# A hybrid attention and mLSTM layer on Trainium2: output stored patch by patch, and a smaller scratch for dynamic DMA descriptors

## Chip, cores and metric

The kernel runs on one core of a Trainium2 chip (TRN2). The metric is the device time of one execution in microseconds (us), the median of several runs. Before the change it is 1314.05 us, median of 3 runs (1313.41 to 1314.33).

## What is computed

One layer of a bidirectional encoder, in float32: x has 2048 tokens of 1024 features. The reference, cut to what matters:

```python
mod = silu(c) @ w_ada + b_ada
shift, scale, gate = split(mod, 3)
h = rmsnorm(x, norm_w) * (1 + scale) + shift
proj = h @ w_in + b_in                      # columns split between two head groups
na_out = neighbourhood_attention(q, k, v, rpb) * silu(na_z)   # 8 heads of 64, 8x16 window
qk = silu(short_conv(concat([ml_q, ml_k])))
hm = (mlstm_forward + mlstm_backward) * sigmoid(ml_o)         # 4 heads of 128
ml_out = layernorm_per_head(hm) * ml_norm_w * silu(ml_z)
y = concat([na_out, ml_out]) @ w_out
out = rmsnorm(x + gate * y, final_norm_w)   # (1, 2048, 1024)
```

The attention sees the 2048 tokens as a grid of 32 rows by 64 columns. A query attends to a window of 8 rows and 16 columns around it.

## The kernel before

The work is in two phases. Phase 1 builds h, runs the input projection, the convolution and the mLSTM, and leaves queries, values, gates and the mLSTM branch in DRAM scratch tensors (`d_qna`, `d_vna`, `d_zna`, `d_mix`); the keys stay in SBUF. Matrix products are split into three passes of high and low parts (`hhi`, `hlo`, `whi`, `wlo`).

Phase 2 (`phase2`, from L1399) goes over 16 patches of the grid. A patch is 8 rows by 16 columns, 128 queries, which are the 128 partitions of a tile. The host lays the residual x out by patches as well (`x_p`), so that a patch's x is loaded as one block of 128 rows. A patch has four units of two heads each, and a slot handles two units, so that a patch takes two slots. A slot (`slot`, L1741) issues by hand, in this order: scores (`pS`, L1538), softmax (L1546, L1547, L1558), the products with the values of the slot before (`pO`, L1581), transposes of the probabilities (`pT`, L1566), and between them pieces of the output projection of an earlier patch (`y`, L1626), which fill TensorE's queue. The order of all engines is fixed by the code (`manual_schedule`).

POOL's queue carries phase 2's loads: value chunks (`v`, L1466, one transfer for each grid row of a chunk), the gates (`load_z`, L1476, into `zs` and `gtile`), the mLSTM branch (`load_m`, L1483, into `whi_a` or `wlo_a`), and the residual (`load_x`, L1493, into `xr`). Each transfer of POOL waits for the eighth transfer before it on that queue, since eight semaphores are used in turn. SP's queue carries the bias tables (L1510) and, from the fourth pair on, the queries (L1448).

The output projection of a patch (`outproj`, L1603) adds y to x (L1631), squares it (L1633), and has `scale` (L1652) and `store` (L1666) work out the final norm. For 15 patches, `store` scales the patch on VectorE (L1668) and issues one store of 512 KB from POOL (L1669). The last patch (`end`) is handled in halves, to shorten the end: ScalarE scales the left 512 columns and its queue stores them (L1659, L1660), VectorE scales the right 512 and SP's queue stores them (L1661, L1662).

The destination of these stores is a piece of the output in token order, `og[8 * pr : 8 * pr + 8, 16 * pc : 16 * pc + 16, :]` (L1423, L1650): 8 grid rows, which lie 64 tokens apart, of 16 tokens each.

Of the kernel before, what the change touches and what calls it, by code (L numbers as in the profile page):

```python
# [16 lines left out]
D = 1024  # L17
T = 2048
# [3 lines left out]
GRID_W = 64  # L22
# [36 lines left out]
class Kernel:  # L59
# [1339 lines left out]
    def phase2(self):  # L1399
        nc = self.nc  # L1400
# [16 lines left out]
        for b in range(16):  # L1417
            pr, pc = divmod(b, 4)
# [1 line left out]
            rpc = ROWS_PER_CHUNK[nr, nkc]  # L1420
            nch = -(-nr // rpc)
            geo.append((pr, pc, nr, nkc, nr * nkc, rpc, nch))
        og = self.out[0].rearrange("(r c) d -> r c d", c=GRID_W)  # L1423
        vg = self.d_vna.rearrange("(r c) d -> r c d", c=GRID_W)
        L = {b: {} for b in range(16)}
        fnw = []
# [51 lines left out]
        def mix_parts(b):  # L1478
            m = mixes[pos[b] % 2]
            return [m[:, i * D : (i + 1) * D].rearrange("p (c q) -> p c q", c=8) for i in range(2)]  # L1480

        def load_m(b):
            nc.gpsimd.dma_start(mix_parts(b)[1][:, 4:, :].bitcast(F32), self.d_mix[b])  # L1483

        def load_x(b):
            src = self.x_p[b]
            if b == last_b:
                L[b]["x"] = [p.tile([P, 512], F32, tag="v", bufs=6, name=f"xr_{b}_{i}") for i in range(2)]
                for i, x in enumerate(L[b]["x"]):
                    nc.gpsimd.dma_start(x, src[:, 512 * i : 512 * i + 512])  # L1490
                return
            x = flat(self.raw.tile([P, 4, 256], F32, tag=f"raw{pos[b] % 2}", name=f"xr_{b}"))
            nc.gpsimd.dma_start(x, src)  # L1493
            L[b]["x"] = [x[:, 512 * i : 512 * i + 512] for i in range(2)]
            L[b]["row"] = x
# [107 lines left out]
        def outproj(b):  # L1603
            lb = L[b]
            hi, lo = mix_parts(b)
            end = b not in after
            pieces = [slice(0, 512), slice(512, 768), slice(768, 1024)] if end else [slice(0, 512), slice(512, 1024)]
            ssq = few.tile([P, 4], F32, tag="var", bufs=2, name=f"fss_{b}")
            halves = ((4, 5, 6, 7), (0, 1), (2, 3)) if b == b0 else ((4, 5, 6, 7), (0, 1, 2, 3))
            parts = [(i, ks) for ks in halves for i in range(2)]  # L1610
            if end:
                parts += [(2, ks) for ks in halves]
            nxt = after.get(after.get(b))
            ys = {}
            for i, ks in parts:
                cs = pieces[i]
                if i not in ys:
                    finish()
                    ys[i] = self.pp.tile([P, 512], F32, tag="pp", name=f"y_{b}_{i}")[:, : cs.stop - cs.start]
                y = ys[i]  # L1620
                assert (b, ks[0] // 4) in split
                if ks[0] == 0 and i == 0 and nxt is not None:
                    load_m(nxt)
                for k in ks:
                    for n, (m, w) in enumerate(((hi, wohi), (hi, wolo), (lo, wohi))):
                        nc.tensor.matmul(y, m[:, k, :], w[k][:, cs], start=(k == 4 and n == 0), stop=(k == 3 and n == 2))  # L1626
                        if k != 3 or n < 2:
                            yield
                if ks[-1] == 3:
                    x = lb["x"][cs.start // 512][:, cs.start % 512 : (cs.stop - 1) % 512 + 1]  # L1630
                    nc.vector.tensor_add(x, x, y)  # L1631
                    at = i + 3 - len(pieces)
                    square = lambda x=x, y=y, at=at: nc.scalar.activation(y, x, AF.Square, accum_out=ssq[:, at : at + 1])  # L1633
                    if end:
                        square()
                    else:
                        self.squares.append(square)
                    if end and i == 1:
                        nc.vector.tensor_add(ssq[:, 1:2], ssq[:, 0:1], ssq[:, 1:2])
                        nc.vector.tensor_scalar(ssq[:, 1:2], ssq[:, 1:2], 1.0 / D, EPS, ALU.mult, ALU.add)  # L1640
                    if end:
                        nc.gpsimd.tensor_tensor(x, x, fnw[0][:, cs].bitcast(F32), ALU.mult)
                    yield
            L.pop(b)
            done.append(b)
            rst = few.tile([P, 1], F32, tag="rst", bufs=2, name=f"frs_{b}")
            var = few.tile([P, 1], F32, tag="fvar", bufs=2, name=f"fvar_{b}")

            pr, pc = divmod(b, 4)
            to = og[8 * pr : 8 * pr + 8, 16 * pc : 16 * pc + 16, :]  # L1650

            def scale():  # L1652
                if not end:
                    nc.vector.tensor_scalar(ssq[:, 1:2], ssq[:, 1:2], 1.0 / D, EPS, ALU.mult, ALU.add)
                nc.vector.scalar_tensor_tensor(var, ssq[:, 2:3], 1.0 / D, ssq[:, 1:2], ALU.mult, ALU.add)
                self.rsqrt(few, rst, var, f"f{b}")
                if end:
                    left, right = lb["x"]
                    nc.scalar.activation(left, left, AF.Copy, scale=rst)  # L1659
                    nc.scalar.dma_start(to[:, :, : D // 2], left)  # L1660
                    nc.vector.tensor_scalar(right, right, rst, None, ALU.mult)  # L1661
                    nc.sync.dma_start(to[:, :, D // 2 :], right)  # L1662
                else:
                    self.todo += [lambda: None, store]

            def store():  # L1666
                x = lb["row"]
                nc.vector.scalar_tensor_tensor(x, x, rst, fnw[0].bitcast(F32), ALU.mult, ALU.mult)  # L1668
                nc.gpsimd.dma_start(to, x)  # L1669
                if nxt not in (None, last_b):  # L1670
                    self.reloads += [lambda: None, lambda: load_x(nxt)]

            if end:
                self.between.append(scale)
            else:
                self.squares.append(lambda: self.between.append(scale))
# [54 lines left out]
        def finish():  # L1731
            while self.squares:
                self.squares.pop(0)()

        def mixed(b, half):
            mix_high(b, half)
            mix_low(b, half)
            if half:
                self.queue.append(outproj(b))
# [67 lines left out]


_INS = ['x', 'x_p', 'x_t', 'cT', 'c_row', 'w_mod', 'w_gt', 'b_ada', 'norm_w', 'w_main', 'w_gate', 'b_col', 'b_row', 'b_gate', 'conv_w', 'conv_b', 'rpb', 'ml_w', 'w_out', 'fnw']
_OUTS = [((1, 2048, 1024), 'float32')]  # L1810


def layout(inputs):
# [71 lines left out]
```

## Time and profile before

| what | value |
|---|---|
| median of 3 runs | 1314.05 us |
| the profiled execution, its own time | 1315.58 us |
| its span, first to last instruction | 1313.8 us |
| mean granted TensorE clock | 0.987 |
| moved by DMA | 263.31 MB, mean 200 GB/s |
| HBM read, written | 177.28 MB, 92.72 MB |

All numbers of the profile are from one execution, whose time is 1.8 us above its span and 1.5 us above the median of the runs. Times of day count from the span's start. PE is TensorE (matmul), PEld its weight load, DVE is VectorE, ACT ScalarE, POOL GpSimd, SP SyncE; SPq and ACTq are the DMA-issuing side of those engines. A row such as "x15, 512.0 KB, 6.8" in the list of DMA issues is a count, the size of one transfer, and the median time from issue to landing in us.

### The profile page before, as it was taken

Reading aid. Unit: us, or ns where it says so; the run is one execution under the profiler, and the core shown is the slowest. Engines: PE = TensorE matmul, PEld = TensorE weight load, DVE = VectorE, ACT = ScalarE, POOL = GpSimd, SP = SyncE. Lnnn points to the kernel's source line nnn. Section 1 sums busy time; section 2 is a strip of 40 time slices with the busy share of each in tenths; the row PEclk is TensorE's granted clock in tenths of the full one; section 3 lists DMA queues with packets and bytes.
Section 4 is the critical chain, followed back from the end, with each engine's and each line's share of the span. In section 5 each row is a group of like instructions: output and inputs, shape, how many; then the busy total and the mean of one; then the engine's idle time right before and its main releaser. Section 6 shows DMA issues by size and latency. Waiting matters only on the chain.

```text
span 1313.8 us, 23067 instructions
## 1 busy us (share of the span) xinstructions
PE 1282.8 (98%) x8170; PEld 1103.1 (84%) x8170; DVE 793.4 (60%) x2394; ACT 531.3 (40%) x1172; POOL 260.6 (20%) x380
## 2 busy tenths in 40 slices
PE   9889999999999999999999999999999999999996
PEld 8889999999888887888888888888777778778785
DVE  5876452112567565166678878767447576766663
ACT  4444243542234222223323323333256555565551
POOL 1400002432000000111212002122305423324431
PEclk7989999999999999999999999999999999999998
DMA  9799955997778764645756767656678756656651
GB/s 363 250 282 305 262 188 152 228 234 202 195 183 186 170 149 110 193 131 165 207 153 209 245 184 215 214 157 183 206 252 261 203 182 194 209 181 194 190 178 48
DMA packets 220662, 263.31 MB, mean 200 GB/s; under 512 B 25463, under 2 KB 165623, under 8 KB 220548
## 3 DMA queue, kind: packets, MB, share of 16 engines
q1 hardware_dynamic: 142526, 189.92, 50.1%
q10 hardware_dynamic: 63270, 35.75, 9.6%
q0 software_dynamic: 14752, 36.17, 9.4%
q8 instruction: 65, 1.06, 0.3%
q14 instruction: 49, 0.40, 0.1%
HBM read 177.28 MB, written 92.72 MB: 206 GB/s over the span
## 4 chain that ended last, share of the span: by engine, by line
PE 80%; issue 4%; DVE 3%; DMA 3%; ACT 1%; POOL 1%; POOLq 0%; ACTq 0%; SPq 0%; DVEq 0%
PE pq L1046 23%; PE y L1626 11%; PE pc L605 4%; PE pc L606 4%; PE pc L604 4%; PE pO L1581 3%; PE pT L1566 3%; PE pvo L604 3%; PE pvo L606 3%; PE pvo L605 3%; PE pS L1538 2%; PE pv L606 2%; PE pv L605 2%; PE pv L604 2%; PE pi L1285 2%
## 5 line engine op out<-in xcount | busy, mean ns | idle before, releaser
L1046 PE MATMUL pq<-hhi,whi_a 128*128 128x512 f32 x512 | 208.4, 407 | 0.9 <-ACT u L951 0.9
L1046 PE MATMUL pq<-hlo,whi_a 128*128 128x512 f32 x512 | 208.2, 407 | 0.0
L1046 PE MATMUL pq<-hhi,wlo_a 128*128 128x512 f32 x512 | 206.7, 404 | 0.0
L1046 PEld LDWEIGHTS pq<-hhi,whi_a 128*128 128x128 f32 x512 | 96.8, 189 | 17.5 <-ACT u L951 1.3
L1046 PEld LDWEIGHTS pq<-hhi,wlo_a 128*128 128x128 f32 x512 | 96.7, 189 | 16.9 <-POOL wlo_a L1020 0.4
L1046 PEld LDWEIGHTS pq<-hlo,whi_a 128*128 128x128 f32 x512 | 96.8, 189 | 16.1 <-issue 0.5
L1020 POOL TENSOR_TENSOR wlo_a<-rawq,whi_a 128x1024 fp32r<-128x1024 f32 x19 | 45.6, 2399 | 293.3 <-ACT whi_a L1019 281.6
L1568 ACT ACTIVATE pt<-pT 96x384 f32<-96x384 f32 (+3 forms) x128 | 65.8, 514 | 87.3 <-PE pT L1566 85.1
L1547 ACT ACTIVATE pbuf<-pbuf,mn 128x480 f32<-128x480 f32 (+5 forms) x128 | 75.9, 594 | 47.8 <-DVE mn L1546 47.8
L1626 PE MATMUL y<-hhi,whi_a 128*128 128x512 f32 x256 | 91.6, 420 | 0.5 <-ACT whi_a L1596 0.5
L1626 PE MATMUL y<-hhi,wlo_a 128*128 128x512 f32 (+1 forms) x272 | 90.6, 399 | 0.2 <-ACT y L1633 0.2
L1466 POOL DMA_DIRECT2D v<-d_vna x158 | 81.8, 523 | 45.0 <-PE pO L1581 17.0
L1288 ACT ACTIVATE num<-px,gtile 128x129 f32<-128x129 f32 x120 | 38.3, 366 | 113.1 <-PE px L1283 80.4
L1546 DVE CUSTOM_DVE_ANT_0 pbuf<-pS,tab 128x480 f32<-128x480 f32 (+5 forms) x128 | 61.8, 539 | 32.3 <-PE pS L1538 32.3
L1307 POOL TENSOR_TENSOR hm<-hm,ck 128x128 f32<-128x128 f32 x64 | 27.5, 429 | 250.6 <-DVE hm L1306 218.5
L1566 PEld LDWEIGHTS pT<-ident,pbuf 128*128 128x128 f32 (+2 forms) x416 | 51.1, 136 | 23.2 <-ACT pt L1568 5.7
L1566 PE MATMUL pT<-ident,pbuf 128*128 128x128 f32 (+2 forms) x416 | 67.0, 274 | 3.0 <-DVE pbuf L1558 2.1
L604 PE MATMUL pvo<-whi_b,hhi 128*128 128x256 f32 x224 | 63.9, 285 | 0.7 <-DVE gates L678 0.7
L606 PE MATMUL pvo<-whi_b,hlo 128*128 128x256 f32 x224 | 63.1, 282 | 0.0
L605 PE MATMUL pvo<-wlo_b,hhi 128*128 128x256 f32 x224 | 63.1, 282 | 0.0
L893 ACT ACTIVATE dec<-dec,gtile 128x128 f32<-128x128 f32 x128 | 41.3, 391 | 49.2 <-POOL dec L886 46.4
L676 DVE TENSOR_TENSOR stvo<-pvo,brow 128x256 f32<-128x256 f32 x60 | 24.8, 419 | 57.6 <-PE pvo L606 44.9
(334 smaller groups left out, 3371.8 us busy)
## 6 DMA issues: line engine op xcount, KB each, us to landing
ck<-d_ck SPq DMA_DIRECT2D x64, 384.5 KB, 3.5
rawq<-in_w_main_dram SPq DMA_DIRECT2D x28, 512.0 KB, 4.5
raw<-in_w_main_dram SPq DMA_DIRECT2D x18, 512.0 KB, 6.1
kv<-d_ck SPq DMA_DIRECT2D x64, 128.5 KB, 2.8
dec<-d_mneg SPq DMA_DIRECT2D x32, 256.0 KB, 5.5
d_ck<-dec ACTq DMA_DIRECT2D x32, 256.0 KB, 7.2
d_qna<-qst ACTq DMA_DIRECT2D x32, 256.0 KB, 4.6
d_ck<-stvo SPq DMA_DIRECT2D x15, 514.0 KB, 4.8
```

Of the source, the lines that this page charges most:

```text
L604: nc.tensor.matmul(ps, lhi(k), rhi(k), start=(k == 0), stop=False)
L605: nc.tensor.matmul(ps, lhi(k), rlo(k), start=False, stop=False)
L606: self.mark = nc.tensor.matmul(ps, llo(k), rhi(k), start=False, stop=(k == KT - 1))
L893: nc.scalar.activation(t[:, o, :], t[:, o, :], AF.Exp, bias=self.cols["g"][:, d, h, c : c + 1])
L1020: (eng or nc.gpsimd).tensor_tensor(lo[:, :, cs], raw, hi[:, :, cs].bitcast(F32), ALU.subtract)
L1046: self.mark = nc.tensor.matmul(patch_ps(ps) if patch else ps, w, self.htok(h, g, k, patch), start=(k == 0 and n == 0), stop=(k == KT - 1 a ...
L1466: queue.dma_start(chunks[key][r * nkc : (r + 1) * nkc, :], rows[r])
L1546: nc.vector.tensor_tensor_reduce(pt[:, :nk], ps, tabs[place[u]][:, j * nk : (j + 1) * nk], 1.0, 3e38, ALU.add, ALU.min, mn)
L1547: nc.scalar.activation(pt[:, :nk], pt[:, :nk], AF.Exp, bias=mn, scale=-1.0, accum_out=sums[:, j : j + 1])
L1566: nc.tensor.transpose(ps[:cs, i, :], U[u][j][:, i * cs : (i + 1) * cs], self.ident)
L1568: nc.scalar.activation(t[:cs, :nch, :], ps[:cs, :nch, :], AF.Copy)
L1626: nc.tensor.matmul(y, m[:, k, :], w[k][:, cs], start=(k == 4 and n == 0), stop=(k == 3 and n == 2))
```

## The change

The output tensor gets the shape of the patches: 16 patches of 128 rows by 1024. Every store then names the patch's block, 128 rows one behind the other in DRAM, and the host puts the patches in their places after the run, outside the timed part. This concerns 17 DMA instructions: 15 from POOL, which now name 128x1024 where they named 8x16x1024, and the last patch's two, 128x512 where they named 8x16x512. The bytes are the same, and so is what each partition sends.

The second part sets the size of the scratch for dynamic DMA descriptors, an area of SBUF at address 0, to 4096 bytes of each partition. The parameter was left at its default before, 16384. Tiles that were placed from the end of that area upward now lie 12288 bytes lower; the freed room is not used.

No instruction moves: on each of the five engines the program has the same instructions in the same order with the same waits, and only the shape of those 17 transfers differs.

```diff
-        og = self.out[0].rearrange("(r c) d -> r c d", c=GRID_W)
...
-            pr, pc = divmod(b, 4)
-            to = og[8 * pr : 8 * pr + 8, 16 * pc : 16 * pc + 16, :]
+            to = self.out[b]
...
-                    nc.scalar.dma_start(to[:, :, : D // 2], left)
+                    nc.scalar.dma_start(to[:, : D // 2], left)
                     nc.vector.tensor_scalar(right, right, rst, None, ALU.mult)
-                    nc.sync.dma_start(to[:, :, D // 2 :], right)
+                    nc.sync.dma_start(to[:, D // 2 :], right)
...
-_OUTS = [((1, 2048, 1024), 'float32')]
+_OUTS = [((16, 128, 1024), 'float32')]
...
-    nc = _bacc.Bacc("TRN2", target_bir_lowering=False, num_devices=1)
+    nc = _bacc.Bacc("TRN2", target_bir_lowering=False, num_devices=1, dynamic_dma_scratch_size=4096)
...
-    return r.results[0]["out_0_dram"]
+    return r.results[0]["out_0_dram"].reshape(4, 4, 8, 16, D).transpose(0, 2, 1, 3, 4).reshape(1, T, D)
```

## The prediction

> **What bounds the kernel now.** I read the page's engine rows first, then a table by stage (busy time of each engine between chosen moments), because the change touches only the last stage. The first row is from the page; the others have, after the stretch and its length, the busy time of PE, PEld, DVE, ACT and POOL, the granted clock, the DMA share and GB/s.
>
> ```profile
> PE 1282.8 (98%) x8170; PEld 1103.1 (84%) x8170; DVE 793.4 (60%) x2394; ACT 531.3 (40%) x1172; POOL 260.6 (20%) x380
> ```
> ```profile
> 1020.50:1123.00 102.50, 102.50 (x774) 81.75 (x773) 67.91 (x225) 57.71 (x151) 34.12 (x64) 1.00 0.65 195
> 1123.00:1205.00 82.00, 82.00 (x620) 65.25 (x619) 55.18 (x180) 47.16 (x120) 25.34 (x47) 1.00 0.64 196
> 1205.00:1302.30 97.30, 97.10 (x706) 78.65 (x704) 59.38 (x201) 47.14 (x132) 34.94 (x63) 1.00 0.52 155
> 1302.30:1313.80 11.50, 0.00 (x0) 0.00 (x0) 2.68 (x11) 1.23 (x3) 0.72 (x1) 0.67 0.16 46
> ```
>
> The first patch's store is issued at 1020.6 us. From there to 1302.3 us TensorE is busy in 281.6 of 281.8 us at full clock, so nothing that the patch stores do in that stretch holds it up. The waits of PE from 1020 us on have one row in all:
>
> ```profile
> PE y L1626 <- ACT y L1633: 0.2, 1, 0.2
> ```
>
> What TensorE does not cover is the last 11.5 us. The timeline of the end gives its order (start, duration, engine, line):
>
> ```profile
> 1302.00 0.28 PE L1626 MATMUL y<-hhi,wlo_a 128*128 128x256 f32 x1
> ...
> 1305.50 0.72 ACT L1659 ACTIVATE xr<-xr,frs 128x512 f32<-128x512 f32 x1 [2.16 <-issue]
> 1305.53 0.49 DVE L1661 TENSOR_SCALAR xr<-xr,frs 128x512 f32<-128x512 f32 x1
> 1306.04 0.68 SPq L1662 DMA_DIRECT2D out_dram<-xr  x1
> 1306.26 0.69 ACTq L1660 DMA_DIRECT2D out_dram<-xr  x1
> ```
>
> After the last matmul the norm of the last patch takes until 1306.0 us; then two stores of 256 KB go out, one from SP and one from ACT, and no engine computes any more. What ends the program is their landing, as the waits of SP's queue from 1300 us on say (total, times, longest):
>
> ```profile
> SPq L1881 <- DMA out_dram<-xr: 4.3, 2, 3.0
> SPq L1881 <- PEq L1881: 2.0, 2, 1.5
> ```
>
> Slices of 1 us show the transfer; the last two columns are the busy share of the 16 DMA engines and the rate.
>
> ```profile
> 1306.00:1307.00 1.00, 0.00 (x0) 0.00 (x0) 0.01 (x1) 0.23 (x1) 0.00 (x0) 0.62 0.00 0
> 1307.00:1308.00 1.00, 0.00 (x0) 0.00 (x0) 0.00 (x0) 0.00 (x0) 0.00 (x0) 0.50 0.39 47
> 1308.00:1309.00 1.00, 0.00 (x0) 0.00 (x0) 0.00 (x0) 0.00 (x0) 0.00 (x0) 0.50 0.42 109
> 1309.00:1310.00 1.00, 0.00 (x0) 0.00 (x0) 0.00 (x0) 0.00 (x0) 0.00 (x0) 0.50 0.51 186
> 1310.00:1311.00 1.00, 0.00 (x0) 0.00 (x0) 0.00 (x0) 0.00 (x0) 0.00 (x0) 0.50 0.47 182
> 1311.00:1312.00 1.00, 0.00 (x0) 0.00 (x0) 0.00 (x0) 0.00 (x0) 0.00 (x0) 0.50 0.00 0
> ```
>
> The share sticks at about a half although nothing else is in flight: eight of the sixteen engines carry the two stores. The DMA view of the window from 1305 us on, 8.8 us long, says the same in packets:
>
> ```profile
> DMA packets 272, 0.52 MB, mean 60 GB/s; under 512 B 16, under 2 KB 16, under 8 KB 272
> ...
> q1 hardware_dynamic: 136, 0.26, 12.3%
> q10 hardware_dynamic: 136, 0.26, 8.0%
> ```
>
> Each store is 128 packets of 2 KB and 8 small ones, which fits one closing packet from each of eight engines, and the pattern that the store names is 8 grid rows by 16 columns. By the Trainium skill ("DMA: Bandwidth & Descriptors", section "Why a DMA increments its semaphore by 16 and not by 1") a transfer is spread over the largest number of engines up to 16 that divides the outermost dimension of both sides, which makes 8 of 8x16 rows against 128 partitions and 16 of 128 rows against 128; the trace's share of 0.5 and its 8 small packets agree for the shape before.
>
> **The last two stores (on the path).** After the change each names 128 rows by 512, like the patch-sized stores elsewhere in the kernel. Their work today is 12.3% and 8.0% of 16 engines over 8.8 us: 0.123 x 16 x 8.8 = 17.3 and 0.080 x 16 x 8.8 = 11.3 engine-us, 28.6 together, which on eight engines is 3.57 us, the stretch that the slices show. The second store is the steady pace, 11.3/128 = 88 ns a packet; the first has 6.0 engine-us more, a slow start of 0.75 us on each of its eight engines. On sixteen engines there are two ends. If the start's 6.0 engine-us are shared out too, the stretch is 28.6/16 = 1.79 us, a saving of 1.79. If each of the sixteen pays the 0.75 us itself, it is 22.6/16 + 0.75 = 2.16 us, a saving of 1.41. A third estimate is from other stores of 256 KB:
>
> ```profile
> d_zna<-qst ACTq DMA_DIRECT2D x16, 256.0 KB, 3.1
> out_dram<-xr POOLq DMA_DIRECT2D x15, 512.0 KB, 6.8
> xr<-in_x_p_dram POOLq DMA_DIRECT2D x15, 512.0 KB, 4.4
> v<-d_vna POOLq DMA_DIRECT2D x94, 48.0 KB, 5.0
> v<-d_vna POOLq DMA_DIRECT2D x64, 64.0 KB, 6.4
> ```
>
> The first row, a store of 128x512, lands 3.1 us after its issue: SP's would be in at 1306.0 + 3.1 = 1309.1, ACT's half behind it 128 x 0.088/16 = 0.7 later, 1309.8 against about 1311.0 now: a saving of 1.2. I take 1.6, between the two ends worked from these very stores, and keep 1.2 to 1.8 for the range. What is late next is the same thing in a smaller size; the norm's chain ahead of it (1302.3 to 1306.0) and the 2.8 us between the last packet and the end of the span are not touched.
>
> A rule would make the gain smaller: by the Trainium skill ("DMA: Bandwidth & Descriptors", section "Anatomy of one DMA — SWDGE (gpsimd) path") a transfer costs about 2.0 us and its bytes at 436 GB/s, given there for POOL's transfers, so that 0.524 MB take an estimated 1.20 us on all engines, 2.40 on half of them, and the spread saves 1.2. The trace does not agree with that rate: it would be 75 ns a packet on each engine, and the steady store takes 88. I stay with the rows.
>
> **The fifteen stores from POOL (beside the path).** They land in 6.8 us where a load of the same 512 KB lands in 4.4; I expect the 4.4 after. Behind a store on POOL's queue stand the next patch's loads, and each transfer there waits for the eighth before it, so some v loads wait for the store:
>
> ```profile
> POOL v L1466 <- DMA out_dram<-xr: 8.8, 8, 2.3
> ```
>
> These 8.8 us of POOL mostly go, and the loads start up to 2.3 us earlier. Nobody on the path was late for them (the 0.2 us above), so I book nothing. The cover is the distance between load and use. The tightest place that I found is the last chunk of the four loads at 997.8 us, used by the batch of pO matmuls at 1013.4; then the landing times of all v transfers (min/median/max):
>
> ```profile
> 997.83 2.00 POOL L1466 DMA_DIRECT2D v<-d_vna  x4 [0.40 <-DMA wlo_a<-d_mix]
> ```
> ```profile
> 1013.37 1.46 PE pO L1581 x24
> ```
> ```profile
> DMA to landing us min/median/max: 2.1/5.8/7.8
> ```
>
> The last of the four is issued at 997.83 + 1.5 = 999.3 and used 14 us later; even the slowest landing, 7.8, leaves 6 us.
>
> **The scratch of 4096 bytes.** Only POOL's transfers use it. Every engine's instructions stand in the same order with the same waits; the tiles from address 0 up lie 12 KB lower. The trace shows no wait that I can put down to the scratch, so I bound its cost from below by 0 and from above by the second rival; a gain is excluded on the path, since TensorE waits for nothing there. I take 0: one hold of POOL, even of a store's whole 6.8 us, would about fit into the 6 us that the tightest load has, and elsewhere there is more.
>
> **Sum.** The profiled execution took 1315.58 us with a span of 1313.8; 1.6 less is 1313.98, span 1312.2. The median of the runs, 1314.05, is 1.5 under the profiled time; on its scale 1314.05 - 1.6 = 1312.45, I say 1312.4. What counts as a change here is 0.2%, 2.63 us, about what a measurement of this kernel can tell from none; the saving is 0.12%.
>
> **Rivals.** *The spread does not come* (chance 0.14): the two final stores stay on eight engines, because the pattern is merged or split in another way than I read, or sixteen engines are slowed by what they write to. Against it is the 3.1 us of the 128x512 store. It gives 1314.05.
>
> *More than the spread* (0.09): the first store's slow start vanishes, so that the stretch falls to 22.6/16 = 1.41 us (saving 2.16), and a third of the 2.8 us after the last packet goes too, since each engine closes half as much: 3.1 in all, 1311.0. It becomes measurable from 0.5 us of that wait on. Nothing in the profile speaks for that second part.
>
> *The small scratch starves POOL* (0.07), the slower side. If a quarter of the scratch holds fewer transfers than must be in flight, POOL's loads come late and every patch waits. The four POOL rows above sum to 94 x 5.0 + 64 x 6.4 + 15 x 4.4 + 15 x 6.8 = 1048 us of landing. They are issued between these moments:
>
> ```profile
> L1466 POOL DMA_DIRECT2D v<-d_vna x158: 496/505/746, 931.5 to 1258.5; - x158
> ```
> ```profile
> 1295.73 0.62 POOL L1669 DMA_DIRECT2D out_dram<-xr  x1 [12.54 <-DVE xr L1668]
> ```
>
> That is 364 us, 2.9 in flight on average. With room for only two, they need 524 us: +160, 1474 us. It decides below three. Against it: over 228 transfers POOL's queue moved few packets each,
>
> ```profile
> q0 software_dynamic: 14752, 36.17, 9.4%
> ```
>
> 14752/228/16 = 4.0 on an engine, so that what is in flight is small. By the Trainium skill ("DMA: Bandwidth & Descriptors", sections "Terms" and "SWDGE vs HWDGE vs iDMA") a descriptor has 16 bytes and the software queue's rings lie in that scratch, which would leave 256 entries a ring and no starvation; no run here shows it.
>
> **How the numbers follow.** The forecast has 0.70: the other three have 0.30. Its own range is 1312.2 to 1312.9 by the savings of 1.2 to 1.8, and the runs shown lie 0.64 below to 0.28 above their median. With the rival of no effect it reaches up to 1314.05 + 0.28, rounded to 1314.4; down I take it to the 1311.0 of the third case. That leaves out the starved POOL, and more besides only if a size is off. Faster by over 0.2% is the wide gain alone, 0.09; slower the starved POOL, 0.07; the rest, 0.84, is within.
>
> **What would show it.** Right: after 1306 us the share of the DMA engines goes to about 0.9 and is zero by 1309.5; each of the two stores has 16 small packets instead of 8; POOL's stores land in about 4.4 us; the stretch to 1302.3 is the same within 0.5 us. Wrong: the share still at 0.5 (no spread), packets at twice the duration each (the writes are the limit), PE idle before pO or y with POOL's loads landing late (the scratch), or a change of the span ahead of 1302 us of over 1 us, for which I have no reason.

## The result and the profile after

The median is 1309.62 us (13 runs, 1308.01 to 1313.04) against 1315.13 us for the kernel before (13 runs, the three of the first table among them, 1311.80 to 1320.31). The ratio is 0.9957 with an interval of 0.9944 to 0.9970: 5.6 us less, by the interval 3.9 to 7.4. The prediction had said 1.6 us less. The profiled execution took 1308.24 us with a span of 1306.5.

The timeline of the end (start, duration, engine, line) and the slices of 1 us behind it, whose last two columns are the busy share of the 16 DMA engines and the rate:

```profile
1302.78 0.34 SPq L1660 DMA_DIRECT2D out_dram<-xr  x1
1302.99 0.36 ACTq L1658 DMA_DIRECT2D out_dram<-xr  x1
```
```profile
1303.00:1304.00 1.00, 0.00 (x0) 0.00 (x0) 0.00 (x0) 0.00 (x0) 0.00 (x0) 0.52 0.38 141
1304.00:1305.00 1.00, 0.00 (x0) 0.00 (x0) 0.00 (x0) 0.00 (x0) 0.00 (x0) 0.50 1.01 377
1305.00:1306.50 1.50, 0.00 (x0) 0.00 (x0) 0.00 (x0) 0.00 (x0) 0.00 (x0) 0.50 0.01 4
```

All sixteen engines are busy, and the stores are through soon after 1305. Call the time from the issue of SP's last store to the end of the span the tail: it was 1313.8 - 1306.0 = 7.7 us and is 1306.5 - 1302.8 = 3.7. That is 4.0 us, inside the measured interval, near its lower end; that the rest of the 5.6 us belongs to the change is not shown. The 4.0 us have two parts. The first is the stores. The DMA view of the last 8.8 us has 16 small packets for each store and no slow start any more (8.0% for both queues, where the first had 12.3%):

```profile
DMA packets 288, 0.52 MB, mean 60 GB/s; under 512 B 32, under 2 KB 32, under 8 KB 288
...
q1 hardware_dynamic: 144, 0.26, 8.0%
q10 hardware_dynamic: 144, 0.26, 8.0%
```

This is 0.16 x 16 x 8.8 = 22.5 engine-us, 1.41 us on sixteen engines, against 3.57 us on eight. The issue also takes 0.34 us where it took 0.68. The second part is in a view that the prediction did not open: the instructions that close the program, all of one source line (durations in ns: shortest, median, longest; then first and last start). Before:

```profile
L1881 POOLq EVENT_SEMAPHORE  x4: 17/17/17, 1313.0 to 1313.7; - x4
L1881 POOLq DRAIN  x3: 51/98/9590, 1303.4 to 1313.5; - x3
L1881 SPq DRAIN  x3: 7/7/7, 1311.6 to 1313.2; - x3
```

After:

```profile
L1879 POOLq EVENT_SEMAPHORE  x4: 17/17/17, 1305.7 to 1306.4; - x4
L1879 POOLq DRAIN  x3: 51/93/4519, 1300.1 to 1306.2; - x3
L1879 SPq DRAIN  x3: 7/7/7, 1305.6 to 1305.9; - x3
```

POOL's first closing drain starts when its last multiplication (L1642) has been handed over. Before, it took 9.59 us and ended at 1303.38 + 9.59 = 1312.97, while SP had seen both stores land by 1311.6: the end waited 1.4 us for POOL. POOL's next closing instruction, the first EVENT_SEMAPHORE, follows its drain at 1313.0. After, the drain takes 4.52 us and ends at 1304.6, a full 1.0 us before SP is through, and POOL's EVENT_SEMAPHORE follows SP at 1305.7. So the stores' landing, from SP's issue, went from 1311.6 - 1306.0 = 5.6 us to 1305.6 - 1302.8 = 2.8, and what lies behind it from 1313.8 - 1311.6 = 2.2 us to 1306.5 - 1305.6 = 0.9: 4.1 us by these rounded times, 4.0 by the spans. SP's waits after 1295 us show the same two (compare the 4.3 and 2.0 us of before):

```profile
SPq L1879 <- DMA out_dram<-xr: 1.9, 2, 1.3
SPq L1879 <- PEq L1879: 0.7, 2, 0.5
```

The second row names PE's queue, but before, PE had been done since 1302.3 us: the longest wait of that row there, 1.5 us, was for POOL's drain. The 0.7 us that are left after are not the drain, which is over by then, but the closing steps behind SP; the kernel with the small scratch alone shows the same 0.7.

**Ahead of the tail** the profile of after is 3.3 us early (last matmul at 1298.74 us, before 1302.00). That is no gain of the change, as the experiments below show. In both kernels an early group of matmuls shows the lead already (the last times are its first and last start), and the stretch from 10 to 32 us (busy time of PE and so on, granted clock behind POOL) shows where it arises. Before:

```profile
L659 PE MATMUL pvo<-whi_a,hhi x96: 283/289/595, 72.6 to 136.6; 128*128 128x272 f32 x96
```
```profile
10.00:32.00 22.00, 20.82 (x110) 20.41 (x111) 15.76 (x34) 10.10 (x19) 3.52 (x2) 0.61 1.01 390
```

After:

```profile
L659 PE MATMUL pvo<-whi_a,hhi x96: 283/288/595, 68.3 to 132.2; 128*128 128x272 f32 x96
```
```profile
10.00:32.00 22.00, 21.93 (x158) 21.38 (x159) 18.51 (x37) 11.92 (x21) 4.54 (x3) 0.84 1.02 390
```

The 4.3 us of lead at 68 us go with how soon TensorE is granted its clock (0.61 against 0.84 in this stretch, 110 against 158 matmuls), and 3.3 of them are left at the end. Two kernels below that differ only in 1 KB of scratch lie 5.3 us apart at this group. Single runs of the kernel before spread from 1309.19 to 1318.28 us in one session; a start that differs by chance fits that, but each kernel has one profile, so it is not shown for single runs. I compare tails in the profiles, and times only over many runs. The patch stores from POOL land in 2.9 us instead of 6.8, and the v loads behind them no longer wait for them; as forecast, TensorE does not notice (its waits from 1016 us on):

```profile
out_dram<-xr POOLq DMA_DIRECT2D x15, 512.0 KB, 2.9
v<-d_vna POOLq DMA_DIRECT2D x94, 48.0 KB, 4.3
v<-d_vna POOLq DMA_DIRECT2D x64, 64.0 KB, 4.6
```
```profile
PE y L1625 <- ACT y L1632: 0.2, 1, 0.2
```

### The profile page after: what moved, and what is told of

It is laid out like the page before. It is cut to its first block, busy times and chain, and to the rows that moved or that the text cites. A ratio compares the mean times of both kernels' runs of the same rounds, so it can differ in the third digit from the quotient of the medians.

```text
span 1306.5 us, 23067 instructions
## 1 busy us (share of the span) xinstructions
PE 1279.6 (98%) x8170; PEld 1098.8 (84%) x8170; DVE 794.3 (61%) x2394; ACT 531.1 (41%) x1172; POOL 258.2 (20%) x380
```

## The experiments

Theory A: the program ends when the later of two things is over, the last two stores and POOL's closing drain; the stores' part comes from the sixteen engines, and the drain is shortened by the small scratch. Rival B: all is the stores', and the drain only waits for them. Rival C: the smaller scratch, which moves the tiles, gained the 3.3 us ahead of the tail. The table sums up what follows; "drain" and "tail" are from the profile, the ratio to the kernel before is of timed runs (blank where a kernel was run only once).

| kernel | scratch | last stores | drain, us | tail, us | ratio (interval) |
|---|---|---|---|---|---|
| before | 16384 | 8x16 rows | 9.59 | 7.7 | 1 |
| the change | 4096 | 128 rows | 4.52 | 3.7 | 0.9957 (0.9944 to 0.9970) |
| stores alone | 16384 | 128 rows | 9.59 | 7.7 | 1.0009 (0.9991 to 1.0027) |
| scratch alone | 4096 | 8x16 rows | 2.56 | 6.4 | 0.9990 (0.9974 to 1.0005) |
| 8 groups, 72 KB apart | 4096 | 8x16 rows | 2.57 | 6.4 | 0.9991 (0.9972 to 1.0010) |
| 16 groups, 512 KB apart | 4096 | 16x8 rows | 4.52 | 4.6 | 0.9972 (0.9954 to 0.9991) |
| 16 groups, 36 KB apart | 4096 | 16x8 rows | 4.53 | 4.5 | |
| early drain | 16384 | 128 rows | 9.37 | 3.7 | 0.9967 (0.9952 to 0.9982) |
| merged loads | 16384 | 128 rows | 5.01 | 3.7 | |
| scratch of 13312 | 13312 | 128 rows | 9.58 | 7.7 | |
| scratch of 12288 | 12288 | 128 rows | 9.58 | 7.7 | |
| scratch of 8192 | 8192 | 128 rows | 3.21 | 3.7 | |
| scratch of 1024 | 1024 | 128 rows | 1.42 | 3.7 | 0.9967 (0.9947 to 0.9987) |

### The stores alone

```diff
-    nc = _bacc.Bacc("TRN2", target_bir_lowering=False, num_devices=1, dynamic_dma_scratch_size=4096)
+    nc = _bacc.Bacc("TRN2", target_bir_lowering=False, num_devices=1)
```

> Only the stores are changed (output by patches, scratch left at its default). Measure: the tail, from the issue of SP's last store to the end of the span, 7.7 us before and 3.7 us after. Theory A (the end waits for the later of two things, the last stores and POOL's closing drain, and the drain's 9.6 us goes with the scratch): the stores land as early as after, but the drain still takes 8.4 to 9.6 us from 2.7 us ahead of the store's issue, so the tail stays at 6.5 to 7.7 us and the time is within 1.2 us of before. Rival B (all of the tail's gain is the stores', the drain only waits for them): drain about 4.5 us, tail 3.7 us, time 4 us under before.

The closing instructions of this kernel, then SP's waits after 1295 us:

```profile
L1879 POOLq DRAIN  x3: 51/93/9586, 1300.6 to 1310.7; - x3
L1879 SPq DRAIN  x3: 7/7/7, 1306.1 to 1310.4; - x3
```
```profile
SPq L1879 <- PEq L1879: 4.7, 2, 4.2
SPq L1879 <- DMA out_dram<-xr: 1.9, 2, 1.3
```

The wait for the stores is 1.9 us as in the changed kernel, SP is through at 1306.1, and then everything stands still until POOL's drain ends at 1310.1. What the stores save, the wait labelled PEq takes: tail 7.7 us, ratio 1.0009. B falls: the drain is as long as before (9.586 against 9.590 us) though the stores were in 4 us before its end, where before they were in 1.4 us before it. The prediction's whole saving is worth nothing by itself.

### The scratch alone

```diff
-    nc = _bacc.Bacc("TRN2", target_bir_lowering=False, num_devices=1)
+    nc = _bacc.Bacc("TRN2", target_bir_lowering=False, num_devices=1, dynamic_dma_scratch_size=4096)
```

(on the kernel before)

> Only the scratch is changed to 4096, the stores name 8x16 rows in token order as before. Theory A: POOL's closing drain takes about 4.5 us and is no longer last; the two stores still run on eight engines and end the program, tail 6.3 us, time 1.4 us under before. Rival B: drain near 9.6 us, tail 7.7 us, time as before. Rival C (the smaller scratch, by moving the tiles, gained the 3.3 us that the profile of after is ahead of before's when the last store is issued): the last store is issued near 1302.8 us in this profile as well, and in that of the stores alone near 1306.0; if instead it is chance in the TensorE clock of the first 30 us, the two differ as the clock of their first 30 us does.

```profile
L1881 POOLq DRAIN  x3: 51/98/2564, 1305.9 to 1314.6; - x3
```
```profile
SPq L1881 <- DMA out_dram<-xr: 4.2, 2, 3.0
SPq L1881 <- PEq L1881: 0.7, 2, 0.5
```
```profile
10.00:32.00 22.00, 21.92 (x124) 20.98 (x124) 13.58 (x31) 9.71 (x18) 3.25 (x2) 1.00 1.03 394
```

The drain is out of the way and the stores on eight engines end the program: SP waits 4.2 us for them, as before, and the row labelled PEq falls from 2.0 to 0.7. The tail is 6.4 us, 1.4 less than before, as A said. A had the drain at 4.5 us; it is 2.56, so the size of the scratch is not all that it goes by. C falls as well: the last store is issued at 1308.55 us here, later than before's 1306.04, with 124 matmuls from 10 to 32 us. (The 1.00 in this row's clock column is no measure: this trace's clock records begin only at 24.5 us.) The ratio of 0.9990 fits a gain of 1.4 us, though its interval reaches over 1.

### How the stores' shape counts

```diff
-            to = self.out[b]
+            to = self.out[b, :, :16]
...
-_OUTS = [((16, 128, 1024), 'float32')]
+_OUTS = [((16, 8, 18, 1024), 'float32')]
```

Eight groups of 16 rows, close together (scratch 4096; the output is padded, the host takes the rows out, and the slices of the last patch's two stores change to match):

> Scratch 4096; the stores keep the shape of 8x16 rows but go to a padded patch block, whose 8 groups lie 72 KB apart instead of 256 KB. It tells the number of engines from the far rows. Engines (the stretch of the two stores was long because eight engines carried them): DMA share 0.5, 8 small packets in a store, stretch 3.3 to 3.8 us, tail 6.0 to 6.4 us. Far rows (the first store's slow start came from the 256 KB pitch): the start's 0.75 us go, the second store behind it as before, stretch 2.8 us, tail 5.5 us.

```profile
q1 hardware_dynamic: 136, 0.26, 12.3%
q10 hardware_dynamic: 136, 0.26, 8.0%
```

The two rows of the last 8.8 us are those of before, 8 small packets and the slow start, tail 6.4 us. The distance of 256 KB had no part in it.

```diff
-            to = self.out[b]
+            to = self.out[:, b]
...
-_OUTS = [((16, 128, 1024), 'float32')]
+_OUTS = [((16, 16, 8, 1024), 'float32')]
```

Sixteen groups of 8 rows, 512 KB apart:

> Scratch 4096; the stores name 16 groups of 8 rows that lie 512 KB apart. Engines: 16 small packets in a store, DMA share near 1.0, stretch 1.5 us, tail 3.7 us, as after. Far rows: a slow start as before, the first store's packets over 100 ns in the mean, stretch 2.2 us or more, tail 4.4 us or more.

Then the same groups 36 KB apart, in a padded output (`self.out[b, :, :8]` of `(16, 16, 9, 1024)`):

> As the kernel with 16 groups of 8 rows 512 KB apart, but the groups lie 36 KB apart. It tells the shape from the distance in what that kernel kept: an issue of 0.60 us, a first store whose packets take 126 ns in the mean (87 in the changed kernel), a tail of 4.6 us. By the shape (a store of groups and rows costs the queue more than one of rows): the same three numbers. By the distance: issue as there, but packets of 87 ns and a tail of about 4.1 us.

The last 8.6 us of the one and of the other:

```profile
DMA packets 288, 0.52 MB, mean 61 GB/s; under 512 B 32, under 2 KB 32, under 8 KB 288
...
q1 hardware_dynamic: 144, 0.26, 11.9%
q10 hardware_dynamic: 144, 0.26, 8.7%
```
```profile
q1 hardware_dynamic: 144, 0.26, 11.9%
q10 hardware_dynamic: 144, 0.26, 8.6%
```

Both run on sixteen engines (16 small packets each) and both keep the slow start, an issue of 0.60 us and a tail of 4.5 to 4.6 us. Neither the engines nor the distance make the slow start: it belongs to stores that name groups and rows. Of the 6.4 - 3.7 = 2.7 us that the stores are worth with the small scratch, the number of engines makes 6.4 - 4.55 = 1.8 us and the plain shape 4.55 - 3.7 = 0.9. By the Trainium skill ("DMA: Bandwidth & Descriptors", section "Why a DMA increments its semaphore by 16 and not by 1") the outermost dimension sets the number of engines; the 8 and 16 small packets of these shapes agree.

### Where the drain starts

```diff
-                        nc.gpsimd.tensor_tensor(x, x, fnw[0][:, cs].bitcast(F32), ALU.mult)
+                        nc.vector.tensor_tensor(x, x, fnw[0][:, cs].bitcast(F32), ALU.mult)
```

(on the kernel with the stores alone, scratch at its default)

> Stores by patches, scratch at its default, and the last patch's three multiplications by the norm's weight on VectorE instead of POOL, so that POOL's last work is the fifteenth store, some 7 us before the issue of SP's last store. The drain's length is not touched, only its start. Theory A (the end waits for the later of drain and stores): drain 9.6 us as before, but it starts about 9 us ahead of SP's store and is over when the stores land; tail 3.7 us, time 3.5 us under before (VectorE's multiplications cost up to 0.5 us on the way to the norm). If the drain itself must wait for the last stores or for all engines: tail 7.7 us as with the stores alone.

```profile
L1879 POOLq DRAIN  x3: 51/93/9367, 1295.1 to 1308.9; - x3
L1879 SPq DRAIN  x3: 7/7/7, 1308.4 to 1308.7; - x3
```

The drain is nearly as long as with the stores alone (9.37 against 9.59 us), but it starts behind the fifteenth store and is over at 1304.5 us, before SP's last store is even issued at 1305.5. Tail 3.7 us, ratio 0.9967: the gain without any smaller scratch. So the drain costs by where it ends, and it does not wait for the stores of the other queues. This is A's strongest test. The tail ties with that of the changed kernel, as in all kernels where the plain stores come last.

### What the drain counts

Merged loads (on the kernel with the stores alone): 107 transfers on POOL's queue instead of 228 (the expectations say 225; the traces have 228).

```diff
-                    if b == b0:
-                        queue.dma_start(chunks[key][: n * nkc, :], rows)
-                    else:
-                        for r in range(n):
-                            queue.dma_start(chunks[key][r * nkc : (r + 1) * nkc, :], rows[r])
+                    queue.dma_start(chunks[key][: n * nkc, :], rows)
```

> Stores by patches, scratch at its default, and each value chunk loaded by one transfer instead of one for each grid row: 107 transfers on POOL's queue instead of 225, the same bytes. It tells what the drain's 9.6 us count. By transfers that the queue still holds (9.59/225 = 43 ns each): 4.6 us, tail 3.7 us. By the size of the scratch: 9.6 us, tail 7.7 us.

```profile
L1875 POOLq DRAIN  x3: 51/102/5015, 1305.2 to 1311.3; - x3
```

POOL's queue in the kernel with the stores alone and in this one (packets, MB, share of the engines):

```profile
q0 software_dynamic: 12832, 36.16, 8.3%
```
```profile
q0 software_dynamic: 16496, 36.20, 8.5%
```

The bytes are the same and the packets are more, so the shorter drain goes by neither. With the scratch at its default it goes with the transfers, by these two counts (9.59 - 5.01)/(228 - 107) = 38 ns each, and 1.0 us besides. That leaves why a smaller scratch shortens it. Three runs of the changed kernel with only the size of the scratch changed:

> The changed kernel with a scratch of 8192 bytes. By the size of the scratch alone, on the line through 16384 (9.59 us) and 4096 (4.52 us): 6.2 us. By transfers still held: twice as many as with 4096 if the scratch is full, 9.0 us. Tail: the drain starts 2.7 us ahead of SP's issue and 0.8 us follow, so 4.4 us for a drain of 6.2 and 7.2 us for one of 9.0.

> The changed kernel with a scratch of 12288 bytes. The profile of the changed kernel has 12832 packets on POOL's queue, 802 for each of 16 engines; with 16 bytes for each, 12288 holds 768. Theory (the queue forgets finished transfers only when it needs room, then all of them, and the drain goes over those it still knows, 39 ns each and 0.9 us besides): it runs full once, near the end, so few transfers are left: drain 0.9 to 2.5 us, tail 3.7 us. If the drain goes with the size of the scratch: 7.9 us on the line of 16384 and 4096, tail 6 us.

> The changed kernel with a scratch of 13312 bytes, which holds 832 entries of 16 bytes, more than the 802. Theory of forgetting when full: it never runs full, all 225 transfers are left, drain 9.6 us and tail 7.7 us as with the default, although the scratch is only a twelfth larger than in the kernel with 12288. By size: 8.3 us, tail 6.4 us.

The first closing instruction of the three, 8192, 12288 and 13312:

```profile
L1879 POOLq DRAIN  x3: 51/93/3212, 1304.4 to 1310.5; - x3
```
```profile
L1879 POOLq DRAIN  x3: 51/93/9582, 1305.5 to 1315.6; - x3
```
```profile
L1879 POOLq DRAIN  x3: 51/93/9584, 1298.0 to 1308.1; - x3
```

From 12288 to 16384 the drain stays at 9.58 to 9.59 us, at 8192 it is 3.21, at 4096 it is 4.52. It does not follow the size of the scratch. Two of the three expectations missed: 8192 gave less than either forecast, and 12288 shows no sign of having run full, so the 802 entries against room for 768 were a wrong count. The third, 13312, came out as the theory had it, but after 12288 it tells nothing new. A queue that remembers its transfers until it needs room fits the plateau, the jump below it and the drop to 2.56 us when the same scratch had to serve stores of another shape. But whether it does so, where exactly it forgets, and how much, none of these runs shows; that stays open. The last two also bear on the early lead, by the first group of matmuls, of 12288 and then 13312:

```profile
L659 PE MATMUL pvo<-whi_a,hhi x96: 283/289/595, 73.5 to 137.6; 128*128 128x272 f32 x96
```
```profile
L659 PE MATMUL pvo<-whi_a,hhi x96: 283/289/597, 68.2 to 132.2; 128*128 128x272 f32 x96
```

The lead goes with neither part of the change: with 4096 bytes the group starts at 68.3 us (the change) and 73.7 (scratch alone), with stores of 128 rows at 68.3, 73.5 and 68.2.

### A scratch of 1024

> The changed kernel with a scratch of 1024 bytes, a sixteenth of the default. The prediction's rival of a starved POOL: POOL's loads wait for room; TensorE shows idle time before pO or y, and the time grows by tens of us if fewer than three transfers fit. If a sixteenth still holds what is in flight: POOL's issues and the stage up to the last matmul as in the changed kernel, drain under 2 us, tail 3.7 us since the stores are last already, time as the changed kernel.

```profile
L1879 POOLq DRAIN  x3: 51/98/1416, 1300.8 to 1306.8; - x3
```
```profile
PE pT L1565 <- DVE pbuf L1557: 0.2, 1, 0.2
PE y L1625 <- ACT y L1632: 0.2, 1, 0.2
```

TensorE waits 0.4 us in all from 1000 us on, and the time is that of the other kernels with a tail of 3.7 us. Even a sixteenth of the default starves nobody; a starved POOL, the prediction's rival, shows at no size tried here.

## Why the prediction was wrong

The step that failed is the one on the scratch, "The trace shows no wait that I can put down to the scratch" and "I take 0", together with its twin in the last two stores' part, that "the 2.8 us between the last packet and the end of the span are not touched". The wait was in the prediction's own fence: "SPq L1881 <- PEq L1881: 2.0, 2, 1.5" is 1.5 us of SP waiting for somebody after the stores had landed, on a label whose engine had stopped at 1302.3 us. The prediction read the row above it, and said of both that the landing ends the program. Its reason against a gain from the scratch, "since TensorE waits for nothing there", says nothing of the last 11.5 us, in which TensorE has no work. The view of that line's instructions would have shown the 9.59 us drain, its end at 1312.97, and the bound: with the drain untouched, no saving on the stores could bring the end forward at all. What the runs showed in its place: the stores alone took 0.0 us off the tail, the scratch alone 1.4 and both together 4.0, so that the stores' 2.7 us count only once the drain is out of the way. The right forecast for the stores alone was 0.

Point by point. That TensorE covers everything up to the last matmul held, in every kernel run. That the two last stores ran on eight engines and would run on sixteen held, with share and small packets as forecast. Its size was off: the sum allowed 1.41 to 1.79 us, on the assumption that the first store's slow start is a latency that is shared out or paid again. It is neither; it went with the groups, so that the stretch fell from 3.57 to 1.41 us, 2.16, which was the first half of the rival "more than the spread". Another 0.5 us or so came ahead of the first packet, with the issue of 0.34 us instead of 0.68, on which the prediction had no term. The second half of that rival, a shorter wait after the last packet, came true in size (1.4 us against a guess of 0.9) by luck: it was not each engine closing half as much, it was POOL.

The fifteen POOL stores moved the way that was forecast, and further (6.8 to 2.9 us, where 4.4 was said), and nothing on the path noticed. "The stretch to 1302.3 is the same within 0.5 us" did not hold in the profiles, by 3.3 us, and the prediction had no reason for that: the profiles lie up to some 5 us apart after the first 70 us, whatever the kernel. Single runs of the kernel before spread by 0.7%, so a measurement of this kernel can tell 0.2% only over many runs, and a range built on three runs was too narrow.

## What to carry to other kernels

This program ended with the last of its engines' closing instructions, so ahead of pricing a faster last store, look at what each queue does after its last work and write down when it ends. A wait whose named engine has long been done has another cause: find it before the row is passed over. Issue POOL's last transfer and work early, or give its queue few transfers, since the drain behind them cost 38 ns for each transfer here with the default scratch; and let a store name plain rows, since groups of rows cost a slow start here, and eight of them half of the engines.

## What was not expected of the hardware

POOL's closing drain: 9.59 us for 228 transfers and 5.01 us for 107 with the default scratch, although the last of them had landed 1.6 us (the kernel before) to 4.7 us ahead of it; 1.42 to 4.53 us with 1024 to 8192 bytes, and not in the order of the sizes. The shape of a store: an issue of 0.34 us for 128 rows, 0.60 to 0.70 us for groups of rows, and a first store at 11.9 to 12.3% of the engines' time where plain rows take 8.0%, whatever the distance of the groups. And the start: the profiles of two kernels that differ in nothing but 1 KB of scratch were 5.3 us apart after 70 us; between the kernels before and after, 4.3 us there went with a granted clock of 0.61 and 0.84 from 10 to 32 us.
